# Small parts of the mixer's first 32 weight tiles: made in the mixer, or one stage earlier and kept in DRAM

## The chip, the cores and the metric

One NeuronCore of one Trainium2 chip runs the whole layer. The metric is the device time of one execution in microseconds (us). TensorE (PE) multiplies, VectorE (DVE), ScalarE (ACT) and GpSimd (POOL) do the rest, and SyncE (SP) issues most of the DMAs. Every engine, and every engine's stream of DMA issues, works through its own list of instructions in order: an instruction that waits holds up all that stands behind it in its list.

## What is computed

One encoder layer on 512 tokens of width 1024, all in float32:

```python
x = x + 0.5 * swiglu(rms_norm(x, n1), gate1, up1, down1)   # first block, inner width 2816
h = rms_norm(x, mix_norm); p = h @ w_in                    # mixer, 28 column tiles of w_in
o_a = gdn_mixer(...)     # conv of 5 taps, gated delta rule in chunks, both directions, 4 heads
o_b = dilated_mixer(...) # windowed softmax attention, 8 heads
x = x + concat(o_a, o_b) @ w_out
x = x + 0.5 * swiglu(rms_norm(x, n2), gate2, up2, down2)   # second block
x = rms_norm(x, final)
```

## The kernel before

**Split products.** A float32 product is made of three fp32r products: every weight tile is split into a large part `hi` (ACT copies it to fp32r, L178 or L229) and a small part `lo` (DVE subtracts `hi` from the raw tile, L179 or L226). `mm3` (L232) then issues hi·x_hi, hi·x_lo, lo·x_hi, so the small part is first read by the third matmul of a tile.

**The first block** (`ffn`, L284): 22 pairs of gate and up tiles of 128x1024, then the down projection: 8 output tiles `d`, each from three weight tiles of 1024, 1024 and 768 columns (L320 to L328). `wload` (L167) fetches the raw tile through SP into one of two `wraw` buffers, and splits it into one of two `whi`/`wlo` buffers. After each `d`, `after1` adds the square (ACT, POOL), splits the new x (ACT L272, DVE L273) and writes x to DRAM (`x_d`, L360).

**The mixer** works through the units of `ORDER`: K, Q, V (conv inputs), Z (gate), Pa, Pb (attention q and k) and v (attention values). Each unit is one column tile of `w_in`, read as two weight tiles of 128x512 (`plan`, L186), 24 matmuls in all; tiles 0 to 31 are the 16 units K0 Q0 K1 Q1 K3 Q2 K2 Z0 Q3 V0 Pa0 V1 Z3 V2 V3 v0. `wnext` (L211) holds three tiles `wsp`, whose two halves are hi and lo. The raw tile comes through SP into one of two halves of `wrw` (`fetch`, L198). A `wsp` buffer comes free when PE has used the tile three places earlier.

PE's order in the mixer is written out by a planner (`interleave`, L62): each stream of work yields how long PE is busy and when it is next due. On the other engines the framework's scheduler orders the instructions. Woven into the projections are, per head, the decay matrices (`decay`, L549: factors `gb` by DVE, POOL and ACT, matmuls `pdc`, exponentials `M` on ACT L164) and `gram` (L602): transposes `ptk` and products `pkk`, `pkq` on PE, squares on ACT (L615), masks `itr` on DVE (L638) and POOL (L640), and eight products into `M` on DVE (L643), four for each direction. From `M` eight small DMAs on SP write diagonal blocks to DRAM (`D1`, L649). When all four heads are there, `solve` (L825) reads them back (`MM`, L831), copies them (DVE L832) and runs some 120 short DVE steps (L842, L846). The projections' results leave PSUM through DVE: `xp` (L428), `z` (L584), `qk` (L661). Their buffers are two and are used in turn, so Z3's result `pz` can only begin when Pa0's `pqk`, two units before, has been read by `qk`.

Of the kernel before, what the change touches and what calls it, by code (L numbers as in the profile page):

```python
# [10 lines left out]
F32 = mybir.dt.float32  # L11
F32R = mybir.dt.float32r
AF = mybir.ActivationFunctionType
ALU = mybir.AluOpType
AX = mybir.AxisListType

P = 128
T = 512
# [15 lines left out]
N_MASK = 768  # L34
LV0, LVG, SCG, ATG = 9.0, 0.625, 0.8, 0.55
GIN, VGO, VGV, PRG, NRG, VTG, VBG, OPG, OTG, FNG, SVG, SSD, SST, VTP, LVH, VTS, RDG = 9.5, 16.5, 4.0, 0.5, 6.0, 3.5, 3.5, 13.5, 0.75, 10.5, 0.75, 8.0, 0.6, 3.0, 1.3, 1.6, 2.0
PRI = 0, 1, 2, 4, 3, 5
ORDER = "rs@1 pa@3 K0 ab gt@2 Q0 K1 bi Q1 pc@3 g0 K3 Q2 K2 g1 Z0 g2 Q3 g3 V0 Pa0 V1 Z3 V2 V3 v0 Pb0 Z2 Z1 Pb1 v1 Pa1 v3 Pa2 Pb2 v2 Pb3 Pa3 oa"

# [50 lines left out]
def encoder_layer(ctx, tc, xT, gu1, dn1, win, wab, wo1, wo2, gu2, dn2, cols, relb, masks, onehot, lnc, sel, out):  # L90
    nc = tc.nc
    te, ve, se, gp, sy = PEQueue(tc, nc.tensor), nc.vector, nc.scalar, nc.gpsimd, nc.sync
# [4 lines left out]
    WF = {"pool": None}  # L97
    tp = ctx.enter_context(tc.tile_pool(name="tp", bufs=2))
    ps = ctx.enter_context(tc.tile_pool(name="ps", bufs=2, space=bass.MemoryType.PSUM))
    dr = ctx.enter_context(tc.tile_pool(name="dr", bufs=1, space=bass.MemoryType.DRAM))  # L100
# [18 lines left out]
    def palt(name):  # L119
        nalt[0] += 1  # L120
        return (pmm, pfl, prg)[nalt[0] % 3](name)

    def tmp(tag, name, n=T, dt=F32, bufs=2):
        return tp.tile([P, n], dt, tag=tag, name=name, bufs=bufs)
# [23 lines left out]

    LE = "natural_log_exp_and_others"
    act = {"silu": [], "pre": None}  # L150

    def silu(o, i):
        act["silu"].append(se.activation(o, i, AF.Silu))
# [13 lines left out]
    def wload(src, n, k, low=False, parts=1, then=None):  # L167
        w = n * k
        raw = WF["pool"].tile([P, 1024], F32, tag="raw", name="wraw", bufs=2)
        if low:  # L170
            hi, lo = (wtile(nm) for nm in ("whi", "wlo"))
        else:
            hi, lo = (WF["pool"].tile([P, 1024], F32R, tag=nm, name=nm, bufs=2) for nm in ("whi", "wlo"))
        sv = src.rearrange("p a b -> p (a b)")
        for i in range(parts):
            s = slice(i * w // parts, (i + 1) * w // parts)
            act["lastf"] = sy.dma_start(out=raw[:, s], in_=sv[:, s])
            se.copy(hi[:, s], raw[:, s])  # L178
            ve.tensor_tensor(out=lo[:, s], in0=raw[:, s], in1=hi.bitcast(F32)[:, s], op=ALU.subtract)  # L179
            if then is not None:  # L180
                then(i)
        return (hi[:, :w].rearrange("p (a b) -> p a b", b=k),
                lo[:, :w].rearrange("p (a b) -> p a b", b=k))

    first = {"K": 4, "Q": 0, "V": 8, "Z": 12, "Pa": 16, "Pb": 20, "v": 24}
    plan = [win[first[u[:-1]] + int(u[-1]), :, 4 * i:4 * i + 4] for u in ORDER.split() if u[:-1] in first  # L186
            for i in range(2)]
    plan += [wo1[d, :, 4 * u:4 * u + 4] for d in range(4) for u in range(3)] + [wo2[d] for d in range(4)]
    plan += [gu2[0, j, :, 4 * u:4 * u + 4] for j in range(2) for u in range(2)]
    nw, got, fetched, ready, wraw = [0], [0, 0], [], [], []  # L190

    def wtile(name, dt=F32R):

        nw[0] += 1
        t, n = ("wb", 1) if nw[0] % 4 == 0 else ("wa", 3)
        return wp.tile([P, 1024], dt, tag=t, name=name, bufs=n)

    def fetch(i):  # L198
        if i < len(plan):
            r = wraw[0][:, i % 2 * T:(i % 2 + 1) * T]  # L200
            sy.dma_start(out=r, in_=plan[i].rearrange("p a b -> p (a b)"))
            fetched.append(r)
# [8 lines left out]
    def wnext():  # L211

        while got[0] < len(plan) and len(ready) < 3:
            t = wp.tile([P, 1024], F32R, tag="wa", name="wsp", bufs=3)
            ready.append(t)
            got[0] += 1
        while got[1] < got[0] - (got[0] < len(plan)):
            i = got[1] - got[0] + len(ready)
            split(ready[i][:, 0:T], ready[i][:, T:2 * T], fetched.pop(0))
            got[1] += 1  # L220
            fetch(got[1] + 1)
        t = ready.pop(0)
        return [t[:, i * T:(i + 1) * T].rearrange("p (a b) -> p a b", b=P) for i in range(2)]

    def sub(o, a, b):
        ve.tensor_tensor(out=o, in0=a, in1=b.bitcast(F32), op=ALU.subtract)  # L226

    def split(hi, lo, src):
        se.copy(hi, src)  # L229
        sub(lo, src, hi)  # L230
# [16 lines left out]
    class Norm:  # L247
# [28 lines left out]
        def rstd(self):  # L276
# [4 lines left out]
            preload()  # L281
            rsq(R, pr, 1024.0)

    def ffn(gu, dn, norm, nxt, then=None, late=False, mid=None):  # L284
        with tc.tile_pool(name="wf", bufs=2, reuse_waits="tile") as wf, \
                tc.tile_pool(name="hp", bufs=1, reuse_waits="tile") as hp:
            WF["pool"] = wf
            hh = [hp.tile([P, T], F32R, name=f"hh{f}") for f in range(NF)]
            hl = [hp.tile([P, T], F32R, name=f"hl{f}") for f in range(NF)]
            wait = []  # L290
            for f in range(NF):
                pg, pu = palt("pg"), palt("pu")
                for j, pt in ((0, pg), (1, pu)):
                    if f == 0 and late:
                        for u in (0, 4):
                            wh, wl = wnext()
                            for k in range(u, u + 4):
                                mm3(pt, wh[:, k - u], wl[:, k - u], xh[k], xl[k], k == 0, k == NKT - 1)
                        continue
                    first = then if f == 0 and j == 0 else None  # L300
                    wh, wl = wload(gu[f, j], NKT, P, True, 4 if first else 2 if f == 0 else 1, first)
                    for k in range(NKT):
                        mm3(pt, wh[:, k], wl[:, k], xh[k], xl[k], k == 0, k == NKT - 1)
                wait.append((f, pg, pu))
                if f == (0 if late else 1):
                    with tc.issue_after(norm.last.ins):
                        for k in range(NKT):
                            norm.sq(k)
                    norm.rstd()
                if f == 0 and not late:  # L310
                    continue
                for e, pg, pu in wait:
                    g, u = tmp("g", "g"), tmp("u", "u")
                    ve.tensor_tensor(out=g, in0=pg, in1=R, op=ALU.mult)  # L314
                    silu(g, g)
                    ve.tensor_tensor(out=u, in0=pu, in1=R, op=ALU.mult)  # L316
                    ve.tensor_tensor(out=u, in0=u, in1=g, op=ALU.mult)
                    split(hh[e], hl[e], u)
                wait = []
            for d in range(NKT - 1 if late else NKT):  # L320
                pd = palt("pd")
                for f0, n in ((0, 8), (8, 8), (16, 6)):
                    wh, wl = wload(dn[d, :, f0:f0 + n], n, P)
                    for i in range(n):
                        f = f0 + i
                        mm3(pd, wh[:, i], wl[:, i], hh[f], hl[f], f == 0, f == NF - 1)
                ve.scalar_tensor_tensor(out=x[d], in0=pd, scalar=0.5, in1=x[d], op0=ALU.mult, op1=ALU.add)
                nxt(d)  # L328
            if late:
                d = NKT - 1  # L330
                ws = [wload(dn[d, :, f0:f0 + n], n, P, f0 == 0) for f0, n in ((0, 8), (8, 8), (16, 6))]
                for i in range(2):
                    pd, s = palt("pd"), slice(256 * i, 256 * i + 256)
                    for f in range(NF):
                        wh, wl = ws[f // 8]
                        mm3(pd[:, 0:256], wh[:, f % 8], wl[:, f % 8], hh[f][:, s], hl[f][:, s], f == 0, f == NF - 1)
                        if (i, f) in ((0, 15), (1, 4)):
                            with tc.issue_after(act["mm"].ins):
                                mid(i)
                    ve.scalar_tensor_tensor(out=x[d][:, s], in0=pd[:, 0:256], scalar=0.5, in1=x[d][:, s], op0=ALU.mult,  # L340
                                            op1=ALU.add)
                nxt(d)
# [15 lines left out]
    def after1(d):  # L358
        n2.add(d)
        sy.dma_start(out=x_d[d], in_=x[d])  # L360

    ffn(gu1, dn1, n1, after1, bring)
    with tc.issue_after(act["lastf"].ins):
        sy.dma_start(out=mk, in_=masks)

    wopen()
    with ExitStack() as mctx:
# [845 lines left out]
        ss = [fins(), chain(), after(), norms(), att(), px()]  # L1213
        interleave([ss[i] for i in PRI])
        te.fixed = False
        for d in range(NKT):
# [4 lines left out]
            for i in range(2):  # L1221
                j = 2 * (d % 2) + i
# [125 lines left out]
```

## Time and profile before

| | |
|---|---|
| median of 3 runs | 1105.24 us (1104.09 to 1106.45) |
| the profiled execution | 1104.93 us, of which the span from the first to the last instruction is 1103.2 us |
| mean granted TensorE clock | 0.992 |
| first block | 0 to 369 us, its down projection from about 250 us |
| mixer and output projection | 369 to 729 us |
| second block and final norm | 729 to 1103 us |

The profile gives busy times by engine, and for each instruction what ended the idle time before it. A matmul of 512 columns is listed with 0.39 us, but such matmuls are pipelined and one starts every 0.23 us; PE is idle only where a row names an idle time. An average over the span hides that the stages have different limits, so stretches are read one by one.

### The profile page before, as it was taken

Reading aid. Unit: us, or ns where it says so; the run is one execution under the profiler, and the core shown is the slowest. Engines: PE = TensorE matmul, PEld = TensorE weight load, DVE = VectorE, ACT = ScalarE, POOL = GpSimd, SP = SyncE. Lnnn points to the kernel's source line nnn. Section 1 sums busy time; section 2 is a strip of 40 time slices with the busy share of each in tenths; the row PEclk is TensorE's granted clock in tenths of the full one; section 3 lists DMA queues with packets and bytes.
Section 4 is the critical chain, followed back from the end, with each engine's and each line's share of the span. In section 5 each row is a group of like instructions: output and inputs, shape, how many; then the busy total and the mean of one; then the engine's idle time right before and its main releaser. Section 6 shows DMA issues by size and latency. Waiting matters only on the chain.

```text
span 1103.2 us, 14133 instructions
## 1 busy us (share of the span) xinstructions
PE 1067.6 (97%) x5394; PEld 879.2 (80%) x5394; DVE 614.8 (56%) x1113; ACT 443.4 (40%) x812; POOL 87.0 (8%) x123
## 2 busy tenths in 40 slices
PE   9999999999999999899999988999999999999996
PEld 7888888888888777778789766778888888888886
DVE  4544444443434398898787889675444444532223
ACT  6432222232232256434666666463222222332321
POOL 3000000000111222610000010000000000001001
PEclk9999999999999999989999999999999999999998
DMA  5332222234333133445422142232233323333332
GB/s 193 96 96 96 95 96 97 95 112 148 109 121 119 35 102 101 114 120 159 90 75 94 56 160 75 68 118 83 96 99 96 103 95 105 96 87 102 89 105 77
DMA packets 53235, 112.27 MB, mean 102 GB/s; under 512 B 17984, under 2 KB 20576, under 8 KB 53168
## 3 DMA queue, kind: packets, MB, share of 16 engines
q1 hardware_dynamic: 48976, 99.50, 29.3%
q0 software_dynamic: 2896, 10.25, 2.9%
q10 hardware_dynamic: 1296, 1.63, 0.5%
q8 instruction: 42, 0.69, 0.3%
q14 instruction: 25, 0.20, 0.1%
HBM read 102.39 MB, written 8.96 MB: 101 GB/s over the span
## 4 chain that ended last, share of the span: by engine, by line
PE 81%; DVE 11%; ACT 2%; issue 2%; DMA 1%; POOL 1%; DVEq 0%; SPq 0%; ACTq 0%; POOLq 0%
PE pg L52 22%; PE pd L52 22%; PE pu L52 22%; PE pc L50 3%; PE pd L50 2%; PE pqk L50 2%; DVE wsp L226 2%; PE ps L50 2%; PE pl L50 1%; PE pov L50 1%; PE pout L52 1%; PE pT L50 1%; DVE stp L842 1%; PE pS L50 1%; DMA wrw<-in_win 1%
## 5 line engine op out<-in xcount | busy, mean ns | idle before, releaser
L178 ACT CAST whi<-wraw 128x1024 fp32r<-128x1024 f32 (+1 forms) x138 | 137.5, 999 | 425.8 <-issue 167.6
L179 DVE TENSOR_TENSOR wlo<-wraw,whi 128x1024 fp32r<-128x1024 f32 (+1 forms) x138 | 161.1, 1168 | 135.5 <-ACT whi L178 131.2
L52 PE MATMUL pd<-hh,whi 128*128 128x512 f32 (+1 forms) x374 | 141.2, 378 | 0.0
L52 PE MATMUL pd<-hh,wlo 128*128 128x512 f32 (+1 forms) x374 | 140.9, 377 | 0.0
L52 PE MATMUL pd<-hl,whi 128*128 128x512 f32 (+1 forms) x374 | 140.8, 377 | 0.0
L52 PE MATMUL pg<-xh,whi 128*128 128x512 f32 x344 | 135.2, 393 | 0.7 <-ACT whi L178 0.5
L52 PE MATMUL pg<-xl,whi 128*128 128x512 f32 x344 | 135.0, 392 | 0.3 <-DVE xl L273 0.3
L52 PE MATMUL pg<-xh,wlo 128*128 128x512 f32 x344 | 134.6, 391 | 0.0
L52 PE MATMUL pu<-xh,wlo 128*128 128x512 f32 x344 | 133.8, 389 | 0.0
L52 PE MATMUL pu<-xh,whi 128*128 128x512 f32 x344 | 133.8, 389 | 0.0
L52 PE MATMUL pu<-xl,whi 128*128 128x512 f32 x344 | 133.8, 389 | 0.0
L316 DVE TENSOR_TENSOR u<-pu,R 128x512 f32<-128x512 f32 x44 | 30.4, 691 | 129.5 <-PE pu L52 129.5
L52 PEld LDWEIGHTS pd<-hl,whi 128*128 128x128 f32 x374 | 70.3, 188 | 13.1
L52 PEld LDWEIGHTS pd<-hh,whi 128*128 128x128 f32 x374 | 70.3, 188 | 12.9
L52 PEld LDWEIGHTS pd<-hh,wlo 128*128 128x128 f32 x374 | 70.3, 188 | 12.8
L314 DVE TENSOR_TENSOR g<-pg,R 128x512 f32<-128x512 f32 x44 | 30.4, 692 | 84.7 <-PE pg L52 84.6
L52 PEld LDWEIGHTS pg<-xh,whi 128*128 128x128 f32 x344 | 65.0, 189 | 15.0 <-ACT whi L178 1.2
L52 PEld LDWEIGHTS pg<-xl,whi 128*128 128x128 f32 x344 | 64.9, 189 | 14.9 <-DVE xl L273 1.1
L52 PEld LDWEIGHTS pg<-xh,wlo 128*128 128x128 f32 x344 | 64.8, 188 | 13.9 <-issue 0.2
L229 ACT CAST wsp<-wrw 128x512 fp32r<-128x512 f32 x76 | 47.2, 621 | 71.1 <-DMA wrw<-in_win 27.6
L52 PEld LDWEIGHTS pu<-xl,whi 128*128 128x128 f32 x344 | 64.6, 188 | 13.5
L52 PEld LDWEIGHTS pu<-xh,wlo 128*128 128x128 f32 x344 | 64.6, 188 | 13.3
(296 smaller groups left out, 1692.4 us busy)
## 6 DMA issues: line engine op xcount, KB each, us to landing
wraw<-in_gu SPq DMA_DIRECT2D x84, 512.0 KB, 3.5
wraw<-in_dn SPq DMA_DIRECT2D x32, 512.0 KB, 3.5
wrw<-in_win SPq DMA_DIRECT2D x56, 256.0 KB, 2.7
wraw<-in_dn SPq DMA_DIRECT2D x16, 384.0 KB, 3.1
wrw<-in_wo SPq DMA_DIRECT2D x16, 256.0 KB, 2.6
bw<-vec_d POOLq DMA_DIRECT2D x8, 448.0 KB, 4.0
x<-in_xT SPq DMA_DIRECT2D x8, 256.0 KB, 4.8
x_d<-x SPq DMA_DIRECT2D x8, 256.0 KB, 2.0
```

The costliest lines, as they stand in the source:

```text
L50: self.last = f(*a, **k)
L52: self.last = f(*a, **k)
L178: se.copy(hi[:, s], raw[:, s])
L179: ve.tensor_tensor(out=lo[:, s], in0=raw[:, s], in1=hi.bitcast(F32)[:, s], op=ALU.subtract)
L226: ve.tensor_tensor(out=o, in0=a, in1=b.bitcast(F32), op=ALU.subtract)
L229: se.copy(hi, src)
L314: ve.tensor_tensor(out=g, in0=pg, in1=R, op=ALU.mult)
L316: ve.tensor_tensor(out=u, in0=pu, in1=R, op=ALU.mult)
L842: ve.tensor_tensor(out=t, in0=Zs[:, rs_, s:s + 1].broadcast_to([P, ne, ncol]), in1=Mt[:, s:s + 1, s + 1:SB].broadcast_to([P, ne, ncol]), o ...
```

## The change

For the first `PUT` = 32 weight tiles of the mixer the small part is made in the down projection of the first block. `presplit` loads the raw tile (128x512, through SP, two to three tiles ahead), ACT copies it to a scratch tile `phi`, DVE subtracts in place, and SP writes the result to a DRAM buffer `ws`; the write of one tile is issued at the next call of `presplit`. `share` calls it, and ties these instructions on every engine behind the load, copy and subtraction of the down projection's own tile; over the 24 tiles the 32 parts are spread 2, 1, 1 and so on, 4 in three tiles. In the mixer `wnext` loads the small part from `ws` through SP into the tile's second half when the buffer is allocated; the raw tile is still loaded, and ACT still copies the large part. From tile 32 on all is as before. With `PUTG` = 0 the call among the gate and up tiles makes nothing.

```diff
+PUT, PUTG = 32, 0
@@ wload
-            se.copy(hi[:, s], raw[:, s])
-            ve.tensor_tensor(out=lo[:, s], in0=raw[:, s], in1=hi.bitcast(F32)[:, s], op=ALU.subtract)
+            wlast[:] = (act["lastf"], se.copy(hi[:, s], raw[:, s]),
+                        ve.tensor_tensor(out=lo[:, s], in0=raw[:, s], in1=hi.bitcast(F32)[:, s], op=ALU.subtract))
@@ new
+    ws_d = [dr.tile([P, T], F32, name=f"ws{i}") for i in range(PUT)]
+    made, raws, unsent = [0], [], []
+    def send():
+        i, lo = unsent.pop(0)
+        sy.dma_start(out=ws_d[i], in_=lo)
+    def presplit():
+        i = made[0]
+        made[0] += 1
+        if unsent:
+            send()
+        for n in range(0 if i == 0 else i + 2, min(i + 3, PUT)):
+            raws.append(tmp("xp", "praw", T + 4, bufs=3)[:, 0:T] if n % 4 else
+                        WF["pool"].tile([P, T], F32, tag="praw", name="praw", bufs=1))
+            sy.dma_start(out=raws[-1], in_=plan[n].rearrange("p a b -> p (a b)"))
+        lo = raws.pop(0)
+        hi = WF["pool"].tile([P, T], F32R, tag="phi", name="phi", bufs=1)
+        se.copy(hi, lo)
+        ve.tensor_tensor(out=lo.bitcast(F32R), in0=lo, in1=hi.bitcast(F32), op=ALU.subtract)
+        unsent.append((i, lo))
@@ wnext
+            if got[0] < PUT:
+                sy.dma_start(out=t[:, T:2 * T].bitcast(F32), in_=ws_d[got[0]])
...
-            split(ready[i][:, 0:T], ready[i][:, T:2 * T], fetched.pop(0))
+            raw = fetched.pop(0)
+            se.copy(ready[i][:, 0:T], raw)
+            if got[1] >= PUT:
+                sub(ready[i][:, T:2 * T], raw, ready[i][:, 0:T])
@@ new
+    def share(n):
+        with ExitStack() as es:
+            for i in wlast:
+                es.enter_context(tc.issue_after(i.ins))
+            while made[0] < min(n, PUT):
+                presplit()
@@ ffn, down projection
                     wh, wl = wload(dn[d, :, f0:f0 + n], n, P)
+                    if not late:
+                        share(PUT - (PUT - PUTG) * (23 - 3 * d - f0 // 8) // 24)
@@ after the first block
+    while unsent:
+        send()
```

PE's list of matmuls is the same in both kernels, row by row. The other lists change at the following places, among others. In the rows of the change, line numbers stand 2 to 45 lines higher (L179 is L177 of before, L694 is L649), and the number behind `ws_` less 102 is the tile: `ws_127` is tile 25.

SP, the down projection, from one write of x to the next, before:

```order
L360 DMA x_d<-x_72 128x512
L177 DMA wraw<-in_dn 128x1024 x2
L177 DMA wraw<-in_dn 128x768
L360 DMA x_d<-x_73 128x512
```

and with the change:

```order
L403 DMA x_d<-x_72 128x512
L209 DMA praw<-in_win 128x512
L179 DMA wraw<-in_dn 128x1024
L197 DMA ws_108<-praw 128x512
L209 DMA praw<-in_win 128x512 x2
L179 DMA wraw<-in_dn 128x1024
L197 DMA ws_109<-praw 128x512
L209 DMA praw<-in_win 128x512
L179 DMA wraw<-in_dn 128x768
L197 DMA ws_110<-praw 128x512
L197 DMA ws_111<-praw 128x512
L403 DMA x_d<-x_73 128x512
```

Four loads and four writes of 256 KB have come between the three loads of down weights.

SP in the mixer, from the blocks of the third head to the loads of `MM`, before:

```order
L649 DMA D_2564<-M 32x4x32 x8
L201 DMA wrw<-in_win 128x512 x2
L649 DMA D_2564<-M 32x4x32 x8
L201 DMA wrw<-in_win 128x512 x2
L831 DMA MM<-D_2564 64x1024 x2
```

and with the change:

```order
L694 DMA D_2788<-M 32x4x32 x8
L242 DMA wsp<-ws_125 128x512
L227 DMA wrw<-in_win 128x512
L242 DMA wsp<-ws_126 128x512
L227 DMA wrw<-in_win 128x512
L694 DMA D_2788<-M 32x4x32 x4
L242 DMA wsp<-ws_127 128x512
L694 DMA D_2788<-M 32x4x32 x4
L876 DMA MM<-D_2788 64x1024
L242 DMA wsp<-ws_128 128x512
L876 DMA MM<-D_2788 64x1024
```

Small parts of tiles 23 to 26 now stand behind block writes: tile 23 (V1's second) behind the third head's, tile 25 (Z3's second) behind the first four of the last head, tile 26 (V2's first) behind all of them.

DVE, the end of the last head's gram step, before:

```order
L638 TENSOR_TENSOR itr<-pkq,mk 128x4x128
L434 SCALAR_TENSOR_TENSOR vT<-xp,col,vT 128x512
L623 TENSOR_TENSOR bdec<-c_2560,cs 128x2x4
L643 SCALAR_TENSOR_TENSOR M<-pkk,c_2560,M 128x128 x8
L794 RECIPROCAL t_2572<-ivn 128x16
L661 TENSOR_TENSOR qk<-pqk,R 128x512
```

and with the change:

```order
L479 SCALAR_TENSOR_TENSOR vT<-xp,col,vT 128x512
L668 TENSOR_TENSOR bdec<-c_2784,cs 128x2x4
L688 SCALAR_TENSOR_TENSOR M<-pkk,c_2784,M 128x128 x4
L683 TENSOR_TENSOR itr<-pkq,mk 128x4x128
L839 RECIPROCAL t_2796<-ivn 128x16
L706 TENSOR_TENSOR qk<-pqk,R 128x512
L840 TENSOR_TENSOR t_2796<-t_2796,wk 128x16
L688 SCALAR_TENSOR_TENSOR M<-pkk,c_2784,M 128x128 x4
```

The read of Pa0's result has moved ahead of the last four products into `M`, and the second mask `itr` behind the first four. Besides, no subtraction `wsp` is left on DVE before tile 32. On ACT, the first four factors `gb` of the backward direction (L561), which stood one before and three behind the table loads and `silu` of the first head's k and q, all stand before them now.

## Rows read from the trace of the kernel before

**Rows 1.** The page, busy time of each engine over the whole span.
```profile
PE 1067.6 (97%) x5394; PEld 879.2 (80%) x5394; DVE 614.8 (56%) x1113; ACT 443.4 (40%) x812; POOL 87.0 (8%) x123
```

**Rows 2.** Stretches: busy PE, PEld, DVE, ACT, POOL, clock, DMA share, GB/s.
```profile
400.00:420.00 20.00, 16.66 (x78) 13.00 (x77) 18.80 (x32) 15.22 (x31) 6.60 (x10) 1.00 0.36 114
460.00:480.00 20.00, 15.42 (x58) 12.21 (x57) 17.69 (x37) 8.11 (x22) 9.74 (x13) 0.83 0.49 140
480.00:500.00 20.00, 19.93 (x90) 16.17 (x90) 19.97 (x90) 7.04 (x14) 0.00 (x0) 1.00 0.30 93
```

**Rows 3.** Timeline of PE: start, us, instruction, idle time before and its releaser.
```profile
411.78 0.73 PE L50 MATMUL pdc<-gb,excr 128*128 128x512 f32 x2 [1.52 <-ACT gb L561]
419.82 0.66 PE L50 MATMUL ptk<-mk,kT 128*128 128x128 f32 x4 [1.78 <-ACT M L164]
428.42 0.50 PE L50 MATMUL pdc<-gb,excr 128*128 128x512 f32 x1 [0.41 <-DVE gb L555]
459.02 0.47 PE L50 MATMUL pc<-xh,wsp 128*128 128x512 f32 x1 [0.17 <-DVE xp L428]
464.42 0.39 PE L50 MATMUL pc<-xh,wsp 128*128 128x512 f32 x1
469.39 0.77 PE L50 MATMUL pz<-xh,wsp 128*128 128x512 f32 x1 [4.58 <-DVE t L795]
```

**Rows 4.** Stretches, columns as in Rows 2: after the longest idle time, and in the down projection.
```profile
469.40:475.50 6.10, 6.10 (x15) 4.78 (x15) 5.65 (x11) 2.48 (x4) 2.40 (x4) 0.50 0.60 166
280.00:295.00 15.00, 15.00 (x68) 12.43 (x67) 5.84 (x6) 4.13 (x6) 1.78 (x1) 1.00 0.38 113
```

**Rows 5.** Tile `wsp`: durations min/median/max in ns, first and last start.
```profile
L229 ACT CAST wsp<-wrw x76: 602/621/676, 252.5 to 732.3; 128x512 fp32r<-128x512 f32 x76
L226 DVE TENSOR_TENSOR wsp<-wrw,wsp x76: 670/684/1531, 253.1 to 733.5; 128x512 fp32r<-128x512 f32 x76
```

**Rows 6.** Timeline of DVE around the last gram step.
```profile
450.52 0.68 DVE L226 TENSOR_TENSOR wsp<-wrw,wsp 128x512 fp32r<-128x512 f32 x1
...
458.79 1.28 DVE L226 TENSOR_TENSOR wsp<-wrw,wsp 128x512 fp32r<-128x512 f32 x2
...
466.39 2.15 DVE L643 SCALAR_TENSOR_TENSOR M<-pkk,c,M 128x128 f32<-128x128 f32 x8
...
468.62 0.62 DVE L661 TENSOR_TENSOR qk<-pqk,R 128x512 f32<-128x512 f32 x1
...
479.16 1.12 DVE L832 COPY MM<-MM 64x1024 f32<-64x1024 f32 x1
```

**Rows 7.** Timeline of ACT: the exponential that the second idle time waited for.
```profile
419.19 0.58 ACT L164 ACTIVATE M<-pdc 128x512 f32<-128x512 f32 x1
```

**Rows 8.** Timeline of POOL: the last mask.
```profile
464.75 1.70 POOL L640 TENSOR_TENSOR itr<-itr,M 128x512 f32<-128x512 f32 x1 [0.40 <-DVE itr L638]
```

**Rows 9.** Timeline of SP's issues around it.
```profile
455.88 4.67 SPq L649 DMA_DIRECT2D D<-M  x8
460.64 0.85 SPq L201 DMA_DIRECT2D wrw<-in_win  x2
467.53 3.72 SPq L649 DMA_DIRECT2D D<-M  x8
```

**Rows 10.** DMA issues: count, KB each, median us from issue to landing.
```profile
wraw<-in_dn SPq DMA_DIRECT2D x32, 512.0 KB, 3.5
wrw<-in_win SPq DMA_DIRECT2D x56, 256.0 KB, 2.7
D<-M SPq DMA_DIRECT2D x32, 16.0 KB, 1.7
MM<-D SPq DMA_DIRECT2D x2, 256.0 KB, 4.4
```

**Rows 11.** Timeline in the down projection: SP's loads, and ACT's copy of a loaded tile.
```profile
266.84 11.21 SPq L177 DMA_DIRECT2D wraw<-in_dn  x3
...
275.38 1.05 ACT L178 CAST whi<-wraw 128x1024 fp32r<-128x1024 f32 x1 [4.56 <-PE pd L52]
```

More of the change, by code (lines that the diff above doesn't have):

```diff
@@ L150, in encoder_layer @@
     act = {"silu": [], "pre": None}
+    wlast = []
     def silu(o, i):
@@ L301, in ffn @@
                     wh, wl = wload(gu[f, j], NKT, P, True, 4 if first else 2 if f == 0 else 1, first)
+                    if not late:
+                        share(min(2 * f + j - 5, PUTG))
                     for k in range(NKT):
@@ L323, in ffn @@
                     wh, wl = wload(dn[d, :, f0:f0 + n], n, P)
+                    if not late:
+                        share(PUT - (PUT - PUTG) * (23 - 3 * d - f0 // 8) // 24)
                     for i in range(n):
```

## The prediction

> **What bounds the kernel now.** I read the totals first, then the stretches, then PE's idle times, and last what the engines named there did. The page [rows 1] shows PE busy for 97% of the span and DVE for 56%; by that average there is nothing to win on DVE. The stretches [rows 2] say otherwise for one part of the mixer: from 400 to 420 us DVE is busy 18.80 of 20 us and PE has idle time, from 460 to 480 DVE is busy 17.69 and PE idles again, and from 480 to 500, in the solve, DVE is busy 19.97 while PE keeps going. PE's timeline [rows 3] puts the losses in five places: 1.52, 1.78, 0.41, 0.17 and 4.58 us, 8.46 together. After the longest, the granted clock is 0.50, the lower of its two levels, for 6.10 us of full work [rows 4]; at the upper level that work takes half as long, so 3.05 us more are lost. **11.5 us** is what the part from 405 to 481 us loses, and each place names DVE or ACT.
>
> The longest is named after a tiny DVE instruction (L795), but that one only stands behind the real cause. Z3's result needs the PSUM buffer of Pa0, which `qk` reads at 468.62 [rows 6], long after PE had finished Pa0 (V1, the unit after it, started at 459.02 [rows 3]). `qk` stood on DVE behind two subtractions at 458.79, the taps, and eight products into `M` at 466.39. PE went on 0.77 us after `qk` began.
>
> **What leaves the mixer.** 32 subtractions of 0.68 us [rows 5], 21.9 us of DVE time, all before PE's unit Pb0. They matter only where DVE is late. I price the five idle times, PE's order being the same.
>
> *First, 1.52.* PE waited for the factors `gb` on ACT, of which three stood behind two table loads. They now stand before them, and the small gate steps on DVE that feed them have no subtractions between them. I take 0; the upper bound is 1.52 as now.
>
> *Second, 1.78.* The transposes wait for the exponential of the matmul just before them. At least its own 0.58 us [rows 7] remains, and factors still stand before it on ACT: between 0.6 and 1.8 I take the middle, 1.2.
>
> *Third, 0.41,* a wait for DVE's `gb`: 0.
>
> *Fourth and fifth, 0.17 and 4.58.* Two subtractions of the pair at 458.79 and one in the step before (three times 0.6 us from start to start, half of that pair's 1.28) are gone from in front of `qk`, and four of the eight products, half of 2.15, now stand behind it. That moves `qk` from 468.62 to 465.7 and PE's start of Z3 to 466.5. V1 ended at 464.8 (last matmul 464.42 plus 0.39 [rows 3]), so 1.7 us stay. A new wait inside V1, for the small part of tile 23, lies in these 1.7: its load stands on SP behind the third head's block writes, which end at 460.5 [rows 9], and lands 2.7 us later [rows 10], at 463.2, when V1 (24 matmuls from 459.02, about 0.227 us each) wants it at 462.2. The wait is 1 us, and PE's later end of V1 takes it off the wait for `qk`. No idle time is then near 4.58 us, and the 3.05 us of half clock go too.
>
> **What comes instead: SP.** The loads of small parts queue behind writes that wait for DVE. The first four products of the last head would begin at 466.39 less 1.8 (subtractions) less 0.6 (the mask moved behind), 464.0, and end at 465.1. The four block writes take 0.58 us each (4.67 for eight [rows 9]) and end at 467.5; tile 25's small part lands at 470.2. PE wants it 12 matmuls and the two first ones of the tile after 466.5, at 469.7: **0.5**. The mask moved behind costs POOL up to 1.70 [rows 8], so the last products end at about 468.4, four more writes at 470.7, one load of `MM` goes first (0.6), and tile 26's small part lands at 474.0. PE wants it at 473.5 (466.5 and: Z3 is 5.4 us, four transposes 0.6, two matmuls 0.5, tile 25's wait 0.5): **0.5**. The earlier tiles behind the first two heads' writes come out at about 1 us in hand by the same count, and I give them 0.
>
> Left are 1.2 + 1.7 + 0.5 + 0.5 = 3.9, so PE gains 11.5 - 3.9 = **7.6 us** by the end of Z3. The solve must keep up, since it fills DVE: its second `MM` load waits for the last blocks to land (470.7 + 1.7) and takes 4.4 [rows 10], so the copy `MM` starts at 476.8 instead of 479.16. That is 2.4; four subtractions (tiles 28 to 31) leave the solve, 4 x 0.6 = 2.4; and the first three idle times bring 2.5 (1.52 + 0.58 + 0.41). The solve ends **7.3 us** earlier. What follows waits for both, so I take the smaller, 7.3.
>
> **What comes into the down projection.** 32 copies of 0.62 and 32 subtractions of 0.68 us [rows 5], four of each per output tile of 15 us, in which ACT is busy 4.13 and DVE 5.84 us [rows 4]: 6.6 and 8.6 then. They stand behind the tile's own copy and subtraction, so they delay the next tile's only if they themselves wait. Four loads and four writes of 256 KB add 2.10 MB per 15 us, 140 GB/s to the 113 that take a DMA share of 0.38; at that ratio the share becomes 0.85. A down weight is loaded at 266.84 and wanted by ACT at 275.38 [rows 11], 8.5 us for a landing of 3.5 [rows 10]: 5.0 us in hand cover the transfers queued ahead. Sends wait for their own subtraction, but stand behind the load of a weight. I take 0; below nothing is excluded, since PE has no idle time there to give.
>
> **The sum.** 1104.93 - 7.3 = **1097.6 us** for the profiled execution; it stands 0.3 below the median of 1105.24, which I leave out. A difference under 0.2% (2.2 us) can't be told from no change.
>
> **The rivals.**
> *The small parts come late in the mixer.* If a load behind the blocks takes the 4.4 us of `MM` instead of 2.7, tile 23 costs 1.0 more (0.7 of 1.7 lies in the wait for `qk`), tiles 25 and 26 cost 1.7 each: 7.3 - 4.4 leaves 2.9, or 1102.0; if one wait is again long enough for the half clock, 3.05 are lost, 1105.1. I set the middle, 1103.5. For it: the loads share SP with writes that wait for DVE, and the DMA share rises by a load of 256 KB every 2.7 us. Against it: `wrw` loads stand behind the same writes now and land in 2.7. The Trainium skill (DMA: Bandwidth & Descriptors, Latency and other measured facts) gives HBM's own latency as 0.2 us on average and 2 us at high load; by that these loads would take, as an estimate, 4.5 us, and the time would be this rival's. No row here shows it.
>
> *Nothing moves.* DVE is hidden behind PE as the totals say, and each wait finds another releaser at the same moment (ACT keeps all its copies, POOL its masks): 1104.9. The Trainium skill (Perfetto Trace Analysis, Identifying the Most-Contended Engine) says to work first on the engine with the highest occupancy, which is PE; by that rule this is the outcome, and the sum would be 0 instead of 7.3. The stretches of [rows 2] and the releasers in [rows 3] speak against it. That the change doesn't do its work I exclude, since the lists hold 32 copies and subtractions earlier and none of the 32 on DVE later.
>
> *Slower: the down projection starves.* SP's list now holds eight more transfers per output tile, loads wait for earlier writes to land, and ACT's copy of a part may wait for its load with the next weight's copy behind it. It decides from the point where such a wait eats the 5.0 us in hand. Half a us at each of 24 weight tiles costs 12: 1104.9 - 7.3 + 12 = 1109.6. For it speaks the share of 0.85; against it, that parts are loaded two to three calls ahead.
>
> *More than the sum.* If the second wait shrinks to 0.6, SP adds none, and late waits of the attention stages ease by a few us: 1092.
>
> **How the numbers follow.** Forecast 0.50 (1094 to 1101), late small parts 0.18, nothing 0.11, starving 0.14, more 0.07. Faster by over 0.2%: forecast, more, and half of the late parts, 0.66; within 0.2%: nothing and 0.08 of the late parts, 0.19; slower: starving and 0.01, 0.15. The range of 8 in 10 takes in all but starving and the far end of more: 1090.5 to 1105.5.
>
> **What would show it.** Right: `pd` of the first block without idle time up to 369 us; PE's idle time before the first `pz` of Z3 under 2 us and no half clock there; waits for `wsp` loads under 1 us each at tiles 23, 25 and 26; the copy `MM` some 5 us earlier, the solve's end some 7. Wrong: PE idle for `whi` before 369 us (starving); PE idle before a third matmul of a tile with a DMA as releaser for over 2 us (late parts); the same five idle times (nothing).

## The result: slower, and where the time went

The changed kernel takes 1111.66 us (median of six runs, 1109.26 to 1113.95), the kernel before 1104.87 beside it: a ratio of **1.0061**, interval 1.0046 to 1.0076. It is slower by 0.6%; 1097.6 us was forecast. The profiled execution took 1109.26 us, of which 1107.5 are the span, 4.3 more than before.

The page of the changed kernel, busy time of each engine [rows 1]:

```profile
PE 1071.0 (97%) x5394; PEld 876.9 (79%) x5394; DVE 615.5 (56%) x1113; ACT 460.1 (42%) x844; POOL 87.2 (8%) x123
```

The totals tell nothing: DVE's is the same, since its subtractions only moved, and ACT's grew by the 32 new copies. The place shows where the mixer begins, at the first `pc` matmul. Tile `pc` before (durations in ns, then first and last start):

```profile
L50 PE MATMUL pc<-xh,wsp x192: 387/389/793, 369.3 to 489.3; 128*128 128x512 f32 x192
```

and after:

```profile
L51 PE MATMUL pc<-xh,wsp x192: 387/389/793, 377.0 to 491.2; 128*128 128x512 f32 x192
```

The mixer begins 7.7 us late. From there to the end of the span it was 733.9 us (1103.2 - 369.3) and is now 730.5: 3.4 less. So the down projection **lost 7.7** and all behind it **won 3.4**, where the sum had 0 and 7.3. Stretches of after (columns as in [rows 2]; [rows 4] has 280 to 295 of before; the mixer's work lies 7.7 us later in them than in [rows 2]):

```profile
400.00:420.00 20.00, 20.00 (x90) 15.36 (x90) 16.74 (x36) 12.22 (x23) 5.54 (x12) 1.00 0.58 188
460.00:480.00 20.00, 17.32 (x86) 13.72 (x84) 15.56 (x38) 8.71 (x30) 12.33 (x16) 1.00 0.71 191
...
280.00:295.00 15.00, 14.85 (x66) 12.01 (x65) 6.69 (x8) 5.98 (x9) 1.29 (x1) 1.00 0.70 234
250.00:369.00 119.00, 114.93 (x492) 91.11 (x491) 57.31 (x67) 45.92 (x67) 9.95 (x6) 1.00 0.75 232
```

and the last of these stretches before:

```profile
250.00:369.00 119.00, 119.00 (x526) 98.56 (x525) 44.47 (x43) 32.62 (x41) 10.66 (x7) 1.00 0.37 112
```

From 250 to 369 us PE made 492 matmuls, against 526 before; 34 matmuls at 0.227 us are the 7.7 us. The DMA share is 0.75, not the 0.85 of my estimate. PE's idle times there (two of them, in the timeline) name the two halves of a down weight, `whi` of ACT and more often `wlo` of DVE:

```profile
294.80 0.50 PE L53 MATMUL pd<-hh,whi 128*128 128x512 f32 x1 [0.15 <-ACT whi L180]
...
296.06 0.50 PE L53 MATMUL pd<-hh,wlo 128*128 128x512 f32 x1 [0.53 <-DVE wlo L181]
```

Such a wait costs more than its idle time: behind the second of these a matmul started 0.92 us after the one before it, instead of 0.23. Why the weights were late is seen in SP's own list. What SP waited for from 250 to 369 us (total, times, longest):

```profile
SPq L209 <- DMA ws<-praw: 70.3, 20, 4.7
```

The timeline of SP for one output tile (start, us):

```profile
284.73 0.45 SPq L403 DMA_DIRECT2D x_d<-x  x1
287.87 0.33 SPq L209 DMA_DIRECT2D praw<-in_win  x1
288.29 0.62 SPq L179 DMA_DIRECT2D wraw<-in_dn  x1
288.96 0.42 SPq L197 DMA_DIRECT2D ws<-praw  x1
289.48 5.15 SPq L209 DMA_DIRECT2D praw<-in_win  x2
294.68 0.42 SPq L179 DMA_DIRECT2D wraw<-in_dn  x1
```

A raw tile's load (L209) takes the buffer of the tile four places earlier, and waits until that tile's write (L197) has landed. It stands in front of a down weight's load (L179), which has to wait with it: from 289.48 to 294.68 SP issued two loads of raw tiles and nothing else. The chain that ended last shows the loop this makes:

```profile
278.50 4.37 DMA ws<-praw
...
282.88 0.33 SPq L209
...
283.32 3.81 DMA wraw<-in_dn
...
287.21 0.84 ACT whi L180
...
288.08 0.88 DVE wlo L181
288.96 5.32 DMA ws<-praw
```

A write lands, SP goes on, the weight lands 3.81 us later, ACT copies it at once and DVE subtracts, and the next write goes out behind that. ACT was ahead before: it waited for PE to free `whi` (PE pd, as in [rows 11]). Now it waits for the weight, and the 5 us in hand are gone. The DMA issues from 250 to 372 us (count, KB, median us to landing [rows 10]):

```profile
wraw<-in_dn SPq DMA_DIRECT2D x14, 512.0 KB, 4.6
ws<-praw SPq DMA_DIRECT2D x28, 256.0 KB, 4.5
praw<-in_win SPq DMA_DIRECT2D x26, 256.0 KB, 3.4
```

The Trainium skill (DMA: Bandwidth & Descriptors, Anatomy of one DMA — SWDGE (gpsimd) path) says, in a section on DMAs that GpSimd issues, that a semaphore wait of a DMA happens on the sequencer that issues it, before dispatch. SP's rows show the same for SP: the waiting load's 5.15 us are time of the whole list.

In the mixer, the places of [rows 3] after the change (timeline of PE):

```profile
425.23 0.66 PE L51 MATMUL ptk<-mk,kT 128*128 128x128 f32 x4 [1.51 <-ACT M L166]
...
434.10 0.50 PE L51 MATMUL pdc<-gb,excr 128*128 128x512 f32 x1 [0.68 <-DVE gb L600]
...
472.31 0.47 PE L51 MATMUL pz<-xh,wsp 128*128 128x512 f32 x1 [1.44 <-DVE qk L706]
...
480.54 0.73 PE L51 MATMUL pc<-xh,wsp 128*128 128x512 f32 x2 [1.60 <-DMA wsp<-ws]
```

The first idle time is gone, the longest fell from 4.58 to 1.44, and no half clock is left from 460 to 480 us. That part went as forecast.

### The profile page after: what moved, and what is told of

Read it like the earlier page. It is cut to its first block, busy times and chain, and to the rows that moved or that the text cites. A ratio compares the mean times of both kernels' runs of the same rounds, so it can differ in the third digit from the quotient of the medians.

```text
span 1107.5 us, 14374 instructions
## 1 busy us (share of the span) xinstructions
PE 1071.0 (97%) x5394; PEld 876.9 (79%) x5394; DVE 615.5 (56%) x1113; ACT 460.1 (42%) x844; POOL 87.2 (8%) x123
## 4 chain that ended last, share of the span: by engine, by line
PE 77%; DMA 8%; DVE 8%; ACT 2%; issue 2%; POOL 1%; SPq 1%; DVEq 0%; ACTq 0%; POOLq 0%
PE pu L53 22%; PE pg L53 22%; PE pd L53 15%; DMA ws<-praw 4%; PE pc L51 4%; PE pqk L51 3%; DMA wraw<-in_dn 2%; PE pd L51 2%; PE ps L51 2%; PE pvb L51 1%; PE pl L51 1%; PE pov L51 1%; PE pout L53 1%; PE pz L51 1%; PE pT L51 1%
## 5 line engine op out<-in xcount | busy, mean ns | idle before, releaser
L53 PEld LDWEIGHTS pu<-xh,whi 128*128 128x128 f32 x344 | 64.6, 188 | 13.6
```

The costliest lines, as they stand in the source:

```text
L53: self.last = f(*a, **k)
```

## The experiments

The theory after reading the traces, **order**: SP's wait for a landing write, with a weight's load behind it. The rivals: **bytes** (the transfers themselves slow the weights) and **work** (ACT and DVE are held by the parts). Ratios are to the kernel before on the same chip, with their 95% interval. One table for what follows; the waits are SP's for L209 before the mixer, share and GB/s those from 250 to 369 us:

| kernel | ratio | first `pc` | waits for writes | share, GB/s |
|---|---|---|---|---|
| the change | 1.0061 (1.0046 to 1.0076) | 377.0 | 72.6 us, 21 times | 0.75, 232 |
| down_alone | 1.0080 (1.0047 to 1.0113) | 380.0 | 76.6, 21 | 0.70, 222 |
| look_one | 1.0038 (1.0013 to 1.0063) | 378.8 | 73.7, 22 | 0.72, 228 |
| no_pairs | 1.0023 (1.0000 to 1.0045) | 372.9 | 89.9, 25 | 0.67, 211 |
| single_look_one | 0.9964 (0.9941 to 0.9988) | 369.2 | 0.8, 3 | 0.69, 213 |
| eight_buffers | 0.9976 (0.9960 to 0.9993) | 369.2 | none | 0.78, 248 |
| no_writes | 0.9972 (0.9950 to 0.9993) | 369.2 | 2.3, once | 0.58, 180 |
| pool_queue | 1.0050 (1.0018 to 1.0082) | 374.8 | on GpSimd | 0.77, 245 |
| mixer_alone | 0.9979 (0.9961 to 0.9997) | 369.4 | none | 0.39, 120 |

### The two halves apart

```diff
 mixer_alone
-            while made[0] < min(n, PUT):
+            while made[0] < min(n, 2):
...
-                sy.dma_start(out=t[:, T:2 * T].bitcast(F32), in_=ws_d[got[0]])
+                sy.dma_start(out=t[:, T:2 * T].bitcast(F32), in_=ws_d[0])
 down_alone
-            if got[0] < PUT:
+            if False:
...
-            if got[1] >= PUT:
+            if True:
```

> The mixer's part of the change without the down projection's: only the first two small parts are made in the down projection, and all of the first 32 weight tiles of the mixer load the first of them as theirs (so the small parts of the weights are left out of the result; transfers, sizes and waits are those of the change). The first pc matmul should start where it did before, at 369.3 us plus at most 0.3. Theory (the loss sits in the down projection alone, 7.7 us from the first pc's start of 369.26 and 376.98, and the mixer behind it ran 3.4 us shorter, 730.5 against 733.9): 1101.5 us. Rival (the mixer is worth the 7.3 us of the prediction, and the late end of the down projection spoils 4 of them): 1097.6 us. Rival (loads from memory are no better than VectorE's subtraction): 1104.9 us.

> The down projection's part alone: all 32 small parts are made and written, and the mixer makes its small parts on VectorE as before, so nobody reads what was written. Theory (the down projection loses 7.7 us, whatever the mixer does): the first pc matmul at 377 us, 1112.6 us in all. Rival (the loads of the mixer's tiles from memory, which wait in the same queue near the end of the down projection, are what delays it): the first pc matmul below 373 us, 1108 us or less.

The halves add up within their intervals: 0.9979 times 1.0080 is 1.0059, against 1.0061 for the change. In `down_alone` nobody reads what was written, and the first `pc` still comes at 380.0: the loss is made in the down projection, and the rival that the mixer's loads delay it falls. It is larger than the 7.7 expected, 10.7 in its profile: there PE waited once for 1.82 us (for `whi`, at 346.46 us), and the granted clock behind that, from 349 to 353 us, was 0.61. `mixer_alone` has a span of 1101.8, near the 1101.5 of the theory: its part is worth 1.4 us in that profile and 2.3 by the ratio, far from 7.3 even with the down projection undisturbed.

### Two edits that fail alone

```diff
 no_pairs
-PUT, PUTG = 32, 0
+PUT, PUTG = 32, 8
 look_one
-        for n in range(0 if i == 0 else i + 2, min(i + 3, PUT)):
+        for n in range(0 if i == 0 else i + 1, min(i + 2, PUT)):
 single_look_one: both
```

> Eight of the 32 parts are made in the gate and up projections, so that in the down projection one part comes with each weight, and never two one behind the other. Theory (a part's load stands in SyncE's list behind the write of the part made just before it where two come together, waits some 4.5 us until that has landed, and keeps the next weight's load behind it): the 70 us that SyncE waits for writes fall below 20, the first pc matmul comes at 369.3 to 371 us, and the time is 1101.5 to 1103 us. Rival (the bytes are the bound: three quarters of them still move in the down projection): the first pc matmul at 375 us, 1107 to 1109 us. Rival (ScalarE and VectorE are held by the parts): three quarters of the loss stay too.

> All 32 parts stay in the down projection, with their pairs; only a part's raw tile is loaded one step later (one step ahead of its use instead of two), so that the buffer it takes was written out one step longer ago. Bytes, copies and subtractions are those of the change. Theory (SyncE's wait for the landing of a write, with the weight's load behind it): the waits fall from 70 us to some 20, the first pc matmul comes at 370 to 373 us, 1102 to 1106 us. Rival (bytes): as the change, the first pc at 377 us and 1109 to 1112 us. Rival (ScalarE's copy of a part then waits for the later load, with the copy of the next weight behind it): ScalarE is idle for the raw tile, and the time is that of the change or above it.

Both missed, since my picture of SP's list was wrong. In either run a raw tile's load stands right behind the write that it waits for, as the chain of `no_pairs` shows (a write, the load behind its landing, and the weight's load behind that):

```profile
285.86 4.45 DMA ws<-praw
...
290.33 0.33 SPq L209
...
290.76 0.37 SPq L179
```

Without pairs, loading two ahead still asks for the buffer written in the line before (25 waits of 3.6 us); with pairs, loads do so although they go out one ahead (22 waits). `no_pairs` lost less, 3.6 us instead of 7.7, which bytes explain as well (eight parts fewer in the stage); its profiled execution is the fastest of its twelve, 1105.66 us beside a median of 1110.07. So the two were made together:

> The run without pairs, and its raw tiles loaded one step ahead of their use instead of two. SyncE's list reads the same, line by line (write, raw tile, weight), but the raw tile's buffer is now one whose write went out a whole weight, some 5.9 us, earlier, and no longer the one in the line just before. Bytes, copies and subtractions are those of the run without pairs, which had its first pc matmul at 372.9 us and 89.9 us of SyncE's waits for writes in 25 waits. Theory (SyncE waits for the write's landing, with the weight's load behind it in its list): the waits fall below 30 us, the first pc matmul comes at 369.3 to 370.3 us, and with some 732 us behind it the span is 1101 to 1103 us. Rival (bytes, or the work of ScalarE and VectorE): the first pc matmul stays at 372 to 374 us.

The waits are 0.8 us, the first `pc` is at 369.2, and the kernel is **faster** than before by 0.36%. Its span, 1099.9 us, is somewhat below the range expected. The bytes are those of `no_pairs` (213 and 211 GB/s), and SP's list in the stage reads the same but for the writes of x (`x_d`), which here stand behind a raw tile's load and there in front of it. Order holds; bytes and work fall for 24 parts.

### The change itself, with eight buffers

```diff
-            raws.append(tmp("xp", "praw", T + 4, bufs=3)[:, 0:T] if n % 4 else
+            raws.append(tmp("gu"[n // 2 % 2], "praw") if n % 8 > 3 else
+                        tmp("xp", "praw", T + 4, bufs=3)[:, 0:T] if n % 4 else
```

> The change itself, all 32 parts with their pairs and two steps of lookahead in the down projection, but the raw tiles go round eight buffers instead of four (four more of the scratch buffers that nobody uses in that stage). SyncE's list reads as that of the change in its steady part; bytes, copies and subtractions are the same; only a raw tile's load now takes a buffer whose write went out some two weights earlier. Theory (the round trip of a write, waited for in SyncE's list in front of a weight's load): the 72.6 us of waits for writes fall below 10, the first pc matmul comes at 369.2 to 370 us instead of 377.0, and the span is 1099.9 to 1103 us. Rival (bytes: at a DMA share of 0.75 a weight cannot land in time): the first pc matmul at 374 us or later.

Nothing but the buffers differs, all 32 parts and their pairs stay, and the steady part of SP's list reads line by line as that of the change. The timeline of SP of this run, its steady part:

```profile
292.65 0.33 SPq L179 DMA_DIRECT2D wraw<-in_dn  x1
293.25 1.71 SPq L197 DMA_DIRECT2D ws<-praw  x2
295.34 0.32 SPq L404 DMA_DIRECT2D x_d<-x  x1
295.71 0.42 SPq L210 DMA_DIRECT2D praw<-in_win  x1
296.73 0.33 SPq L179 DMA_DIRECT2D wraw<-in_dn  x1
```

and its stretch of the down projection:

```profile
250.00:369.00 119.00, 119.00 (x527) 98.53 (x526) 59.43 (x69) 48.13 (x72) 12.51 (x18) 1.00 0.78 248
```

PE is never idle, with **more** bytes per us than in the change (248 against 232 GB/s) and with a weight's landing of 5.2 us in the median, longer than the change's 4.6. Bytes and work are refuted here for the whole of the change. The median is 1103.12 us.

### No writes, and another engine's list

```diff
 no_writes
-        sy.dma_start(out=ws_d[i], in_=lo)
+        if i == 0:
+            sy.dma_start(out=ws_d[i], in_=lo)
...
-                sy.dma_start(out=t[:, T:2 * T].bitcast(F32), in_=ws_d[got[0]])
+                sy.dma_start(out=t[:, T:2 * T].bitcast(F32), in_=ws_d[0])
 pool_queue
-        sy.dma_start(out=ws_d[i], in_=lo)
+        gp.dma_start(out=ws_d[i], in_=lo)
...
-            sy.dma_start(out=raws[-1], in_=plan[n].rearrange("p a b -> p (a b)"))
+            gp.dma_start(out=raws[-1], in_=plan[n].rearrange("p a b -> p (a b)"))
```

> The change without the writes of the small parts but for the first, which all 32 tiles of the mixer load as theirs (so the other small parts are left out of the result). A raw tile's load then waits for VectorE's subtraction alone; its bytes stay, 8 MB of writes go. Theory (the round trip of a write in SyncE's list): the down projection is back, the first pc matmul at 369.3 to 370.5 us. Rival (ScalarE's copies and VectorE's subtractions of the parts, or the loads' bytes): the first pc matmul at 374 us or later. This run does not tell bytes from order, since both fall; the two runs beside it do.

> The change with all its pairs and two steps of lookahead, but the raw tiles' loads and the writes of the small parts are issued by GpSimd instead of SyncE: the same bytes in the same stage, and what waits for a landing write now stands in a list with no weight behind it. Theory (order in SyncE's list): SyncE waits for no write before 369 us, the weights' loads go out as VectorE frees their buffers, the first pc matmul comes at 369.3 to 371 us. Rival (bytes: a share of 0.75 of the transfer engines slows each weight's load past its 5 us in hand): the first pc matmul at 375 us or later. Third possibility (GpSimd's issuing itself is slow and the parts fall behind the down projection): the weights are in time and the parts late, seen as waits for wsp in the mixer.

`no_writes` went as order expects: first `pc` at 369.2. `pool_queue` did not: 374.8 lies at the rival's bound. Its profile tells why. Tile `pd`, and the one idle time of PE behind it:

```profile
L53 PE MATMUL pd<-hh,whi x176: 387/389/439, 252.7 to 374.1; 128*128 128x512 f32 x176
```

```profile
370.98 0.50 PE L53 MATMUL pd<-hh,wlo 128*128 128x512 f32 x1 [1.94 <-DVE wlo L181]
```

The down projection began at 252.7 instead of 249.5: 3.2 us went at the kernel's start, for a reason that stays open. From there to the first `pc` it took 122.1 us, against 127.5 in the change and 119.8 before. So with SP free of the waits 5.4 of the 7.7 us came back in these profiles, though the kernel as a whole can't be told from the change (1.0050 and 1.0061); 1.94 of the rest is one wait at the end, where a raw tile was late on GpSimd's list (its chain: write 3.81, load 3.23, then `wlo`), and ACT's copies of the parts waited for raw tiles, 44.8 us in 22 times, with the weights' copies behind them. The round trip is the same, only the list that it holds up has changed. The Trainium skill (DMA: Bandwidth & Descriptors, Issuing engines are not separate DMA queues) says that issuing from several engines only saves the sequencer's time to initiate. Here it took waits out of SP's list, and the stage was 5.4 us shorter in the one profile than in the other; the measurement decides.

### All parts in the gate and up projections

```diff
-PUT, PUTG = 32, 0
+PUT, PUTG = 32, 32
...
-        for n in range(0 if i == 0 else i + 2, min(i + 3, PUT)):
+        for n in range(0 if i == 0 else i + 1, min(i + 2, PUT)):
```

> All 32 parts are made in the gate and up projections, one with each weight, loaded one step ahead; the down projection is that of the kernel before. Theory: no write stands ahead of a weight there for longer than the weight can spare, the first pc matmul comes at 369.3 to 370 us, and the mixer behind it takes the 731 to 732.5 us of the runs so far: span 1100.5 to 1102.5 us, faster than the kernel before by 0.1 to 0.25%. Rival (the parts cost in any stage where PE is never idle, since the weights' loads wait there too): the gate and up projections end later, the first pc matmul above 371 us, and nothing is won.

1101.31 us, **0.9956** (0.9934 to 0.9979): the lowest ratio of all, first `pc` at 369.2. Its interval overlaps that of `single_look_one`: no difference is shown between the two stages for the parts, once no write holds up a weight.

### What becomes of the mixer's lead

`single_look_one` begins the mixer where the kernel before did, so the two can be laid side by side. DVE's timeline of it:

```profile
474.01 1.07 DVE L877 COPY MM<-MM 64x1024 f32<-64x1024 f32 x1 [2.56 <-DMA MM<-D]
...
507.20 1.13 DVE L893 COPY ZZ<-ZZ 128x1024 f32<-128x1024 f32 x1
```

The copy `MM` comes 5.15 us earlier than the 479.16 of [rows 6], and the solve's end 6.4 earlier than before (513.62). The first `pS` is 6.5 earlier (528.1 against 534.6), the first `pT` only 3.1 (537.7 against 540.8). Against this profile of before, the lead is lost in those 10 us. PE's timeline there and the stretches (columns as in [rows 2]):

```profile
531.62 0.66 PE L51 MATMUL pqk<-xh,wsp 128*128 128x512 f32 x1 [1.78 <-ACT wsp L248]
```

```profile
530.00:532.00 2.00, 0.38 (x1) 0.36 (x2) 0.61 (x3) 1.76 (x4) 0.00 (x0) 0.95 0.00 0
532.00:534.00 2.00, 2.00 (x6) 1.37 (x5) 0.89 (x2) 0.09 (x1) 0.00 (x0) 0.50 0.29 98
534.00:536.00 2.00, 2.00 (x43) 1.25 (x44) 0.69 (x2) 0.62 (x1) 0.00 (x0) 0.70 0.50 164
```

An idle time of 1.78 us, and then a clock of 0.50 and 0.70, the lower level for 2.0 and 1.2 us, half of which is lost: 1.6. Together 3.4. On ACT the awaited copy (530.96) stood behind the exponential of `L` (530.24). Its raw tile, the mixer's 44th, is loaded behind the solve's last eight loads in SP's list, and ahead of them in the kernel before. So these eight loads were moved:

```diff
 solve_pool (on single_look_one), before_pool (on the kernel before), gate_pool (on gate_look_one)
-                    sy.dma_start(out=dst[s, :, sb], in_=src[:, b, :].rearrange("m (r c) -> r m c", r=SB))
+                    gp.dma_start(out=dst[s, :, sb], in_=src[:, b, :].rearrange("m (r c) -> r m c", r=SB))
```

> The run of single parts loaded one step ahead, and the solve's last eight loads (M and ZT) issued by GpSimd instead of SyncE. In the runs with the mixer's part of the change the first pS came 6.5 us earlier than before and the first pT only 3.1: TensorE waited 1.8 us for ScalarE's copy of a weight tile's large part, which stands there behind the exponential of L, and ran at half clock behind that; the raw tile's load stands behind those eight loads in SyncE's list, where before it stood ahead of them. Theory (this order of loads gives back 3 us): the wait of pqk for ScalarE goes, the first pT comes at 534 to 535 us instead of 537.7, the span is 1096.5 to 1098 us. Rival (GpSimd issues the loads later and the levels wait for M and ZT): the first pl matmul above 522.1 us, and the span is 1099 us or above. Rival (the give-back has another cause): pqk waits as before, 1099.9 us.

> The control: the kernel before with the same eight loads issued by GpSimd. There no weight tile's load stands behind them in a place where TensorE waits. Theory: nothing, 1103.2 us of span within 0.8 us. Rival (GpSimd's queue is better for these loads in any kernel): 1100 to 1101.5 us, and then what the run beside it gains is not due to the order that the change moved.

> All 32 parts in the gate and up projections, one per weight, and the solve's last eight loads on GpSimd: the version that should beat both kernels. Theory: first pc at 369.2 us, first pT at 534 to 535 us, span 1096.5 to 1098 us, 0.5 to 0.6% below the kernel before. Rival as for the run on the down projection with the same eight loads: 1099 to 1101 us.

`solve_pool` 0.9963 (0.9946 to 0.9981), `gate_pool` 0.9970 (0.9955 to 0.9984), the control 1.0006 (0.9986 to 1.0027): by the ratios nothing is won over the runs without the edit. The profiled span of `solve_pool`, 1097.2 us, lies in its range, that of `gate_pool`, 1100.2, in its rival's, and the control's, 1105.3, is 2.1 above before. The wait for `wsp` is gone, as expected, but the time is not. PE's timeline and stretches of `solve_pool`:

```profile
529.89 0.21 PE L51 MATMUL pl<-tts,M 32*32 32x32 f32 x1 [1.21 <-ACT tts L920]
```

```profile
530.00:532.00 2.00, 2.00 (x49) 1.82 (x48) 1.61 (x6) 0.83 (x3) 0.00 (x0) 0.81 0.36 109
532.00:534.00 2.00, 2.00 (x6) 1.32 (x4) 0.00 (x0) 0.46 (x2) 0.00 (x0) 0.50 0.16 61
534.00:536.00 2.00, 2.00 (x52) 1.55 (x51) 1.25 (x4) 0.61 (x1) 0.00 (x0) 0.84 0.03 8
```

A shorter wait for ACT's `tts` comes in its place, the clock falls all the same, and the first `pT` is at 537.0, 9.2 us behind the first `pS` (9.6 without the edit, 6.2 before). That the order of these loads made the wait is shown; that it made the loss is not.

Nor is it shown that the change's part in the mixer gives anything back here. The profile of before has no half clock between 528 and 548 us, but all thirteen others have some us of it, those of the two kernels included whose mixer makes its small parts as before (the control and `down_alone`). From the solve's end (the start of the copy `ZZ`) to the first `pT`, us:

| profile | solve's end | first `pT` | between |
|---|---|---|---|
| before | 513.6 | 540.8 | 27.2 |
| before_pool, the control | 514.0 | 545.1 | 31.1 |
| down_alone | 524.3 | 555.4 | 31.1 |
| single_look_one | 507.2 | 537.7 | 30.5 |
| all eleven with the mixer's part | | | 29.1 to 32.6 |

PE's wait for `qk` in this stretch, in before and in the control, and the control's clock behind it:

```profile
526.92 0.50 PE L50 MATMUL pqk<-xh,wsp 128*128 128x512 f32 x1 [1.47 <-DVE qk L661]
```

```profile
528.31 0.50 PE L50 MATMUL pqk<-xh,wsp 128*128 128x512 f32 x1 [2.94 <-DVE qk L661]
```

```profile
530.00:532.00 2.00, 2.00 (x43) 1.86 (x43) 1.93 (x4) 1.82 (x4) 0.00 (x0) 0.50 0.93 182
```

So the quick profile of before is the exception, and the 3.4 us that seem to be given back belong to the comparison with it. Counted from the first `pc`, the first `pT` of `single_look_one` is 3.0 us earlier than in before and 7.0 earlier than in the control. Neither of the two is before in every line: the control has its eight loads on GpSimd, `down_alone` its other down projection. What makes the wait and the half clock differ between profiles, and how much of the lead is lost behind the solve, stays open.

## Why the prediction was wrong

**The failed step** is "What comes into the down projection ... I take 0". Its parts were seen singly: the eight more transfers, the 5.0 us in hand, "Sends wait for their own subtraction, but stand behind the load of a weight". What it left out is the raw tile's load, which waits for a write to land and stands in front of the next weight's load; the rows of the lists shown with the change have it there (two `praw`, then `wraw`). I set the 5.0 us against transfers queued ahead. A write's landing of 4.5 us (up to 5.6 in the chain), and the weight's own landing of 4.6 instead of 3.5 behind it, use more than that. The cost was 7.7 us. The rival of the starving down projection named this very wait ("loads wait for earlier writes to land") and gave it 0.5 us on each of 24 tiles, 12 us, and 0.14; 7.7 are 0.32 for each. Its time, 1109.6 us, is near the 1109.26 of the profile by luck: 12 for 7.7 and 7.3 for 3.4 make up for each other. Against it I set that parts are loaded two to three calls ahead, which four buffers turn round: the further ahead a load goes, the sooner it asks for a buffer whose write is still under way.

**The mixer's term** was over-sized: 7.3 forecast, 3.4 in the profile of the change and 3.2 in `single_look_one`. The ratios, which don't hang on one profile, give 2.3 (`mixer_alone`) to 4.9 us (`gate_look_one`) where the down projection lost nothing; of their intervals only that of `gate_look_one` reaches 7.3. Single profiles scatter: from the first `pc` to the end, those with the mixer's part go from 727.6 (`solve_pool`) to 734.4 us (`no_writes`). Point by point:
- First idle time 0: right. Second 1.2: 1.51. Third 0: 0.68.
- Fourth and fifth 1.7: 1.44 and 0.17, and no half clock at Z3: right.
- Tiles 25 and 26, 0.5 each: none and 1.60, at the first tile of V2, in the change. All that is left of idle time is then 5.40 instead of 3.9. The loads of small parts land in 2.9 us in the mixer (median of 29 from 376 to 500 us), near the 2.7 that I took. By the latency of HBM at high load that the Trainium skill gives (DMA: Bandwidth & Descriptors, Latency and other measured facts) it would have been, as an estimate, 4.5; this median doesn't show it.
- `MM` some 5 us earlier, the solve's end some 7: 5.15 and 6.4, without the down projection's loss. Right.
- "What follows waits for both, so I take the smaller": not borne out against the profile of before, where a lead of 6.5 us at the first `pS` was 3.1 at the first `pT`. Against the control it was 7.0 there. So the term was over-sized by the ratios, but where the rest of it went is not shown. The rival "late small parts" had the right size at its better end (2.9 us won) by luck: waits for small parts cost 1.8 us in the change, where this rival has 4.4 on top of the forecast's 1.0.

That DVE's work in the mixer is on the path, against the rival "nothing moves", holds: `mixer_alone`, `eight_buffers`, `single_look_one` and `gate_look_one` are all faster than before, by 0.21 to 0.44%.

## What to carry to other kernels

Where a change adds transfers to an engine's list, don't count only bytes and issue time: ask for each which semaphore it waits for, how long that takes to land, and what stands behind it; a load into a buffer that has just been written out waits for a round trip, and takes the next weight with it. More buffers took such a wait out here, and so did a shorter lookahead with single parts; a longer lookahead in the same buffers was not run, but asks for them sooner. A lead that is won in one stage is worth what the next stages can keep of it: follow it there, by the first instruction of each, before it is put into the sum.

## What the runs showed of the hardware

A write of 256 KB from SBUF to DRAM landed in 4.5 us in the median in the change, beside 232 GB/s of traffic, and the load of as much in 3.4. With eight buffers, at 248 GB/s, it was the other way, 3.7 for the write and 5.5 for the load, so neither figure holds beyond its run. A core moved 248 GB/s over 119 us (share 0.78) with 512 KB loads landing in 5.2 us and PE never idle. And PE's clock was at its upper level, 1.00, in the kernel before from 526 to 542 us, behind an idle time of 1.47 us, while in `solve_pool`, behind a stretch of 32x32 matmuls and an idle time of 1.21 us, it fell to the lower one (0.81, 0.50 and 0.84 from 530 to 536 us). The length of the idle time alone doesn't tell the two apart.
